# Rotary embedding on one core: all loads and stores in one ring, the end of each load run as a DMA of its own

## The chip, the core and the metric

The kernel runs on one core of one Trainium2 chip. The metric is the time of one execution in microseconds (us) on the device; several executions are taken and their median is given. One further execution was profiled; every line of the profile comes from it.

## The reference

The input `x` has 16 batches of 512 rows of 1024 float32 numbers; a row holds 16 heads of 64. `cos` and `sin` are tables of 512 x 32. Every head is rotated by the angles of its row:

```python
x = x.reshape(batch, seq, num_heads, head_dim)
x1, x2 = x[..., :half_dim], x[..., half_dim:]
rotated = np.concatenate([x1 * cos - x2 * sin, x1 * sin + x2 * cos], axis=-1)
```

The result is float32 and as large as `x`: 33.55 MB are read and as many written.

## The kernel before, in words

**Tiling.** The work is cut into 8 slabs of 4 MB (`nslabs`). A slab is two half batches: each of the 128 partitions holds 8 consecutive rows (`rpp`), so 8192 float32 numbers or 32 KB (`W` elements) a partition. Two slabs that follow each other share their two batches; in memory their 32 KB lie side by side, so two slabs can be moved by one DMA with 64 KB a partition. The on-chip tile `room` has 6 places for slabs (`slots`); slab `s` lies in place `s % 6`, so slab 6 takes the place of slab 0 and slab 7 that of slab 1.

**Computation, in place.** Every slab goes through five steps, in one pass or, for the first slab and the last two, in two passes of half a slab. ScalarE (ACT) casts float32 to bf16 into the lower half of the slab's own room (L146). VectorE (DVE) makes two products with the tables (L174), one of them with the halves of each head exchanged, and adds them (L177). ACT casts the sum back to float32 over the slab (L178). The slab is then ready to be stored. The tables are prepared once at the start, by small loads on ACT's queue (L89), a cast on GpSimd (L122), eight matmuls on TensorE (L130) and two copies by DVE (L135).

**Loads.** The dictionary `loads` names the DMAs: slabs 0 and 1 alone, slabs 2 and 3 together, slabs 4 and 5 together, slabs 6 and 7 alone. `load` (L70 to L73) issues those for slabs under 6 on SyncE's queue (SP, queue q1 of the profile), all four at the start. Slabs 6 and 7 are loaded from ACT's queue (q10 of the profile): ACT's program issues load 6 between its work for slabs 3 and 4, load 7 one slab later (`LATE = 3`), and each waits until the slab that had the place, 0 or 1, has landed in memory as output.

**Stores.** `stores` names those: slabs 0, 1, 2, 3 alone, 4 and 5 together, 6 and 7 alone. L182 issues them on SP, each behind the last cast of its last slab. The first stands in SP's queue behind the four loads, which have been issued long before.

**Order.** ACT and DVE run in the order in which the program is written (`manual_schedule`); a cast of the next slab stands ahead of the work on the present one. SP's order before the change comes from the planner and is: loads 0, 1, 2, 4, then stores 0, 1, 2, 3, 4, 6, 7. In what follows a load or store is called by its first slab: load 4 is that of slabs 4 and 5.

**Words.** A DMA of 128 partitions is spread over the core's 16 DMA engines; each moves 8 of the 128 rows, and one such row (32 or 64 KB a partition) is one packet in the profile. A queue is a ring of such packets on every engine.

Of the kernel before, what the change touches and what calls it, by code (L numbers as in the profile page):

```python
# [2 lines left out]

# [4 lines left out]


@with_exitstack  # L10
def kernel(
    ctx: ExitStack,
    tc: tile.TileContext,
    x: bass.AP,
    cos: bass.AP,
    sin: bass.AP,
    num_heads: int,
    out: bass.AP,
):
    nc = tc.nc  # L20
    P = nc.NUM_PARTITIONS

    batch, seq, dim = x.shape
    nh = num_heads
    hd = dim // nh
    half = hd // 2
    bf16 = mybir.dt.bfloat16
    f32 = mybir.dt.float32

    nb = 2  # L30
    slots = 6
    LATE = 3
    nslabs = batch // nb
    G = 2
    rpp = nb * seq // P
    W = rpp * dim
    SP = seq // rpp
    TW = rpp * half

    out_flat = out.rearrange("b s h d -> b s (h d)")  # L40

    singles = ctx.enter_context(tc.tile_pool(name="singles", bufs=1))
    psum = ctx.enter_context(tc.tile_pool(
        name="psum", bufs=1, space=bass.MemoryType.PSUM))


    def dram(t, s, k):
        return bass.AP(tensor=t.tensor,
                       offset=t.offset + s // G * (G * nb * seq * dim) + s % G * W,
                       ap=[[G * W, P], [1, k * W]])  # L50


    def view(t, offset, *dims):
        return dataclasses.replace(t, offset=t.offset + offset,
                                   ap=[t.ap[0], *[list(d) for d in dims]])


    room = singles.tile([P, slots * W], f32, tag="room")
    halves = room.bitcast(bf16)


    def slab(s, k):
        return view(room, s % slots * W, (1, k * W))


    loads = {0: 1, 1: 1, 2: 2, 4: 2, 6: 1, 7: 1}
    stores = {0: 1, 1: 1, 2: 1, 3: 1, 4: 2, 6: 1, 7: 1}


    def load(s):  # L70
        k = loads[s]
        queue = nc.sync if s < slots else nc.scalar
        queue.dma_start(out=slab(s, k), in_=dram(x, s, k))  # L73

    TR = 32
    TQ = seq // TR // rpp
    TC = seq * half // TR
    raw = singles.tile([P, TC], f32, tag="raw")  # L80
    nc.vector.memset(raw, 0.0)  # L81


    def load_tables(queue):
        for i, src in enumerate((cos, sin)):
            to = dataclasses.replace(
                raw, offset=raw.offset + i * raw.ap[0][0],
                ap=[[P // TR * raw.ap[0][0], TR], [1, TC]])
            queue.dma_start(out=to, in_=bass.AP(  # L89
                tensor=src.tensor, offset=src.offset, ap=[[TC, TR], [1, TC]]))  # L90


    load(0)
    load_tables(nc.scalar)
    for s in loads:
        if 0 < s < slots:
            load(s)

    GP = SP // G
    GT = G // TQ
    pick = singles.tile([P, 3 * GT * P], bf16, tag="pick")
    nc.gpsimd.memset(pick, 0.0)  # L104


    def selection(g, h):
        return pick[:, (g * GT + h // TQ) * P:(g * GT + h // TQ + 1) * P]


    for g in range(3):
        for h in range(0, G, TQ):
            part = view(selection(g, h), 0, (GP, P // GP), (1, GP))
            nc.gpsimd.affine_select(  # L114
                out=part, in_=part, compare_op=mybir.AluOpType.not_equal,
                fill=-1.0 if g == 2 else 1.0,
                base=-(1 if g else 0) - h // TQ * (P // TR),
                pattern=[[0, P // GP], [-(G // TQ) * (P // TR), GP]],
                channel_multiplier=1)

    raw_b = singles.tile([P, TC], bf16, tag="raw_b")
    nc.gpsimd.tensor_copy(out=raw_b, in_=raw)  # L122

    tab = {}


    def table(h):
        acc = psum.tile([P, 2 * rpp * hd], f32, tag=f"acc{h}")
        for g, at in ((0, 0), (0, half), (2, rpp * hd), (1, rpp * hd + half)):
            nc.tensor.matmul(  # L130
                view(acc, at, (hd, rpp), (1, half)), selection(g, h),
                view(raw_b, h % TQ * TW, (half, rpp), (1, half)),
                start=True, stop=True)
        tab[h] = singles.tile([P, 2 * rpp * hd], bf16, tag=f"tab{h}", name="tab")
        nc.vector.tensor_copy(out=tab[h], in_=acc)  # L135

    def span(u):
        s, r, n = u
        at, m = s % slots * W + r * dim, n * dim
        return (m, view(room, at, (1, m)), view(halves, 2 * at, (1, m)),  # L140
                view(halves, 2 * at + m, (1, m)))


    def cast(u):
        m, full, low, high = span(u)
        nc.scalar.copy(out=low, in_=full)  # L146

    passes = []
    for s in range(nslabs):
        n = rpp if 1 <= s < nslabs - 2 else rpp // 2
        passes += [(s, r, n) for r in range(0, rpp, n)]


    with tc.manual_schedule(engines={mybir.EngineType.Activation, mybir.EngineType.DVE}):
        cast(passes[0])
        done = 1
        for i, u in enumerate(passes):  # L160
            s, r, n = u
            if i == 0:
                for h in range(G):
                    table(h)
            ahead = len(passes[:rpp // passes[0][2]]) if i == 0 else i + 1
            for v in passes[done:ahead + 1]:
                cast(v)
            done = max(done, ahead + 1)
            if s - LATE + slots in loads and s >= LATE and r == 0:
                load(s - LATE + slots)  # L170
            m, full, low, high = span(u)
            turned = view(low, half, (hd, n * nh), (-half, 2), (1, half))
            for out_, in_, a in ((high, turned, rpp * hd), (low, low, 0)):
                nc.vector.tensor_mul(  # L174
                    out=out_, in0=in_,
                    in1=view(tab[s % G], a + r * hd, (hd, n), (0, nh), (1, hd)))
            nc.vector.tensor_add(out=high, in0=low, in1=high)  # L177
            nc.scalar.copy(out=full, in_=high)  # L178
            if r + n == rpp:
                for t, k in stores.items():  # L180
                    if t + k - 1 == s:
                        nc.sync.dma_start(out=dram(out_flat, t, k), in_=slab(t, k))  # L182


# [1 line left out]
_INS = ['x', 'cos', 'sin', 'num_heads']  # L186
_OUTS = [((16, 512, 16, 64), 'float32')]

_NUMBERS = {'num_heads': 16}


# [26 lines left out]
```

## Time and profile before

| what | value |
|---|---|
| median of 3 executions | 162.21 us (162.21 to 162.39) |
| the profiled execution's own time | 162.0 us |
| its span in the profile | 160.2 us |
| bytes read and written in device memory | 33.69 and 33.55 MB |

The span goes from the first to the last instruction; 1.8 us lie outside of it. In the profile SPq and ACTq are the parts of those engines that issue DMAs; "to landing" is the time from a DMA's issue until all its data has arrived and its semaphore says so. The view of stretches gives, for a stretch of the span, each engine's busy time, then TensorE's clock, the mean busy share of the 16 DMA engines, and GB/s. It books a packet wholly where it begins, so in short stretches the share can be over 1.

### The profile page before, as it was taken

What the parts mean: (1) busy time and instruction counts of PE and PEld (TensorE: products, weight loads), DVE (VectorE), ACT (ScalarE), POOL (GpSimd) and SP (SyncE); (2) the same over time, 40 slices, a digit from 0 to 9 for tenths busy, and PEclk for the clock granted to TensorE, in tenths of its full rate; (3) what the DMA queues carried; (4) which work ended last, traced back from release to release, by engine and by line L of the source; (5) the groups of instructions that cost most, each with busy time, mean ns of one, the idle gap of its engine ahead of it and who ended that gap; (6) DMA issues with size and microseconds to landing.
All of it is one profiled execution on the core that took longest, in us unless ns stands there. A gap on an engine that the chain in (4) does not pass through costs nothing.

```text
span 160.2 us, 170 instructions
## 1 busy us (share of the span) xinstructions
PE 1.9 (1%) x8; PEld 1.1 (1%) x8; DVE 110.1 (69%) x36; ACT 113.2 (71%) x23; POOL 2.1 (1%) x9
## 2 busy tenths in 40 slices
PE   0004000000000000000000000000000000000000
PEld 0002000000000000000000000000000000000000
DVE  1002999999906998999899899997399999000000
ACT  3006939992499999999999999299999991800000
POOL 3001000000000000000000000000000000000000
DMA  7999999979989996999999999999998998999994
GB/s 262 409 409 393 515 401 524 458 327 524 425 360 524 409 376 270 458 450 401 458 450 393 450 466 393 442 442 425 417 532 360 524 409 376 401 458 450 393 442 213
DMA packets 1968, 67.24 MB, mean 420 GB/s; under 512 B 240, under 2 KB 240, under 8 KB 304
## 3 DMA queue, kind: packets, MB, share of 16 engines
q1 hardware_dynamic: 1584, 58.72, 85.8%
q10 hardware_dynamic: 384, 8.52, 12.3%
HBM read 33.69 MB, written 33.55 MB: 420 GB/s over the span
## 4 chain that ended last, share of the span: by engine, by line
ACT 36%; DMA 25%; DVE 21%; issue 4%; SPq 1%; ACTq 0%
DMA room<-in_x_dram 25%; ACT room L178 20%; ACT room L146 17%; DVE room L174 14%; DVE room L177 7%; SPq L73 1%; ACTq L178 0%
## 5 line engine op out<-in xcount | busy, mean ns | idle before, releaser
L174 DVE TENSOR_TENSOR room<-room,tab 128x4096 bf16<-128x4096 bf16 (+1 forms) x22 | 71.7, 3260 | 10.9 <-ACT room L146 10.5
L146 ACT CAST room<-room 128x4096 bf16<-128x4096 f32 (+1 forms) x11 | 56.6, 5155 | 17.1 <-DMA room<-in_x_dram 17.1
L178 ACT CAST room<-room 128x4096 f32<-128x4096 bf16 (+1 forms) x11 | 56.6, 5156 | 6.6 <-DVE room L177 6.6
L177 DVE TENSOR_TENSOR room<-room 128x4096 bf16<-128x4096 bf16 (+1 forms) x11 | 35.9, 3262 | 0.4
L135 DVE CAST tab<-acc 128x1024 bf16<-128x1024 f32 x2 | 2.4, 1219 | 13.6 <-PE acc L130 13.6
L146 ACT ACT_TABLE_LOAD x1 | 1.3, 1283 | 2.6 <-issue 2.6
L130 PE MATMUL acc<-raw_b,pick 128*128 128x256 bf16 x8 | 1.9, 415 | 13.9 <-POOL raw_b L122 13.9
L130 PEld LDWEIGHTS <-pick 128*128 128x128 bf16 x8 | 1.1, 140 | 14.2 <-issue 12.3
L81 DVE MEMSET raw<- 128x512 f32 x1 | 0.5, 485 | 0.9 <-PEq L199 0.9
L114 POOL TENSOR_SCALAR_AFFINE_SELECT pick<-pick 128x128 bf16<-128x128 bf16 x3 | 0.8, 309 | 0.1
L122 POOL CAST raw_b<-raw 128x512 bf16<-128x512 f32 x1 | 0.6, 611 | 11.2 <-DMA raw<-in_sin_dram 11.2
L104 POOL MEMSET pick<- 128x384 bf16 x1 | 0.4, 418 | 0.3 <-POOLq L199 0.3
L199 POOL MEMSET const-float32-0.0<- 128x1 f32 x1 | 0.1, 99 | 0.2 <-issue 0.2
L199 POOL MEMSET const-bfloat16-1.0<- 128x1 bf16 x1 | 0.1, 102 | 0.0
L199 POOL MEMSET const-uint8-127<- 128x1 uint8 x1 | 0.1, 102 | 0.0
L199 POOL MEMSET const-float32-1.0<- 128x1 f32 x1 | 0.1, 99 | 0.0
## 6 DMA issues: line engine op xcount, KB each, us to landing
out_dram<-room SPq DMA_DIRECT2D x6, 4096.0 KB, 33.6
room<-in_x_dram SPq DMA_DIRECT2D x2, 4096.0 KB, 17.1
room<-in_x_dram ACTq DMA_DIRECT2D x2, 4096.0 KB, 24.8
raw<-in_cos_dram ACTq DMA_DIRECT2D x1, 64.0 KB, 7.9
raw<-in_sin_dram ACTq DMA_DIRECT2D x1, 64.0 KB, 11.1
room<-in_x_dram SPq DMA_DIRECT2D x2, 50.5
out_dram<-room SPq DMA_DIRECT2D x1, 28.7
```

The lines of the kernel that those rows point to most:

```text
L73: queue.dma_start(out=slab(s, k), in_=dram(x, s, k))
L81: nc.vector.memset(raw, 0.0)
L104: nc.gpsimd.memset(pick, 0.0)
L114: nc.gpsimd.affine_select(out=part, in_=part, compare_op=mybir.AluOpType.not_equal, fill=-1.0 if g == 2 else 1.0, base=-(1 if g else 0) - ...
L122: nc.gpsimd.tensor_copy(out=raw_b, in_=raw)
L130: nc.tensor.matmul(view(acc, at, (hd, rpp), (1, half)), selection(g, h), view(raw_b, h % TQ * TW, (half, rpp), (1, half)), start=True, sto ...
L135: nc.vector.tensor_copy(out=tab[h], in_=acc)
L146: nc.scalar.copy(out=low, in_=full)
L174: nc.vector.tensor_mul(out=out_, in0=in_, in1=view(tab[s % G], a + r * hd, (hd, n), (0, nh), (1, hd)))
L177: nc.vector.tensor_add(out=high, in0=low, in1=high)
L178: nc.scalar.copy(out=full, in_=high)
L199: nc = _bacc.Bacc("TRN2", target_bir_lowering=False, num_devices=1)
```

## The change

There is no load on ACT's queue any more: all loads and stores of slabs are issued on SP, whose order is now written out too. Loads 0, 1, 2 and 4 are issued first, then stores 0 and 1, then loads 6 and 7, then the other stores.

Loads 4 and 7, the last ones ahead of a store, are cut in two DMAs. The last two rows, 2048 numbers or 8 KB a partition (`TAIL = 2`), are a DMA of their own, 1 MB in all. The store behind each of them (store 0 behind load 4, store 2 behind load 7: `gates`) gets a wait: it is issued only when the first part of that load has landed. The tail's DMA is in the queue by then. Load 6 waits for store 0 to land and load 7 for store 1, as before, but now on SP. The work of ACT, DVE, TensorE and GpSimd is the same, but for the two DMA issues that leave ACT.

```diff
-    LATE = 3
+    TAIL = 2
...
+    gates = {4: 0, 7: 2}
+    opened = {}
+
+    def piece(t, s, a, b):
+        return bass.AP(tensor=t.tensor,
+                       offset=t.offset + s // G * (G * nb * seq * dim) + s % G * W + a,
+                       ap=[[G * W, P], [1, b - a]])
 
     def load(s):
-        k = loads[s]
-        queue = nc.sync if s < slots else nc.scalar
-        queue.dma_start(out=slab(s, k), in_=dram(x, s, k))
+        end = loads[s] * W
+        cut = end - TAIL * dim if s in gates else end
+        for a, b in ((0, cut), (cut, end)):
+            if a < b:
+                done = nc.sync.dma_start(
+                    out=view(room, s % slots * W + a, (1, b - a)),
+                    in_=piece(x, s, a, b))
+                if s in gates and a == 0:
+                    opened[gates[s]] = done.ins
+
+    def store(s):
+        gone = nc.sync.dma_start(out=dram(out_flat, s, stores[s]), in_=slab(s, stores[s]))
+        if s in opened:
+            tc.add_manual_dep(
+                gone.ins, opened[s].name,
+                mybir.DependencyInfo(mybir.DependencyClass.Sync,
+                                     mybir.DependencyReason.DATA),
+                reason="behind the load")
...
-    with tc.manual_schedule(engines={mybir.EngineType.Activation, mybir.EngineType.DVE}):
+    with tc.manual_schedule(engines={
+            mybir.EngineType.Activation, mybir.EngineType.DVE, mybir.EngineType.SP}):
...
-            if s - LATE + slots in loads and s >= LATE and r == 0:
-                load(s - LATE + slots)
...
-                        nc.sync.dma_start(out=dram(out_flat, t, k), in_=slab(t, k))
+                        store(t)
+                if s == 1:
+                    load(6)
+                    load(7)
```

## The prediction

> **What bounds the kernel now.** I read the page's totals first, then its chain, then how full the DMA engines are in chosen stretches, because the totals point to them.
>
> ```profile
> span 160.2 us, 170 instructions
> PE 1.9 (1%) x8; PEld 1.1 (1%) x8; DVE 110.1 (69%) x36; ACT 113.2 (71%) x23; POOL 2.1 (1%) x9
> ...
> DMA packets 1968, 67.24 MB, mean 420 GB/s; under 512 B 240, under 2 KB 240, under 8 KB 304
> q1 hardware_dynamic: 1584, 58.72, 85.8%
> q10 hardware_dynamic: 384, 8.52, 12.3%
> ACT 36%; DMA 25%; DVE 21%; issue 4%; SPq 1%; ACTq 0%
> ```
>
> No compute engine is over 71% busy, but the two queues together fill 98.1% of the 16 DMA engines' time. The chain names ACT first, which misleads: it follows the last cast back, and that cast only has to be done before the queue gets to its store. So I checked how long the last store lay in the queue. The first rows are the time-ordered view and the view of the store's line, both near the end; then stretches, whose last two columns are the mean busy share of a DMA engine and GB/s. A packet is booked wholly in the stretch where it begins, so share times width is the mean length of the one packet per engine that begins there, and GB/s times width is their bytes.
>
> ```profile
> 136.01 3.61 ACT L178 CAST room<-room 128x4096 f32<-128x4096 bf16 x1 [3.56 <-DVE room L177]
> 139.64 0.33 SPq L182 DMA_DIRECT2D out_dram<-room  x1
> DMA to landing us min/median/max: 19.7/19.7/19.7
> ...
> core 0: us, PE busy (x) PEld busy (x) DVE busy (x) ACT busy (x) POOL busy (x), PEclk, DMA share, GB/s
> 62.70:110.00 47.30, 0.00 (x0) 0.00 (x0) 45.61 (x12) 44.27 (x8) 0.00 (x0) 1.00 1.00 433
> 110.00:156.00 46.00, 0.00 (x0) 0.00 (x0) 21.63 (x10) 26.00 (x8) 0.00 (x0) 1.00 1.00 433
> ```
>
> The last store, 4.19 MB, is issued at 139.64 and needs 4.19/0.433 = 9.7 us of engine time, yet lands 19.7 us later: about 10 us lie behind other stores. Compute therefore has some 10 us of cover, and the end is set by the queue. From 62.7 on it moves 433 GB/s without a hole, in the stretch where the two rings mix (62.7 to 110) as in the one with stores alone. 67.24 MB at 433 GB/s are 155.3 us; what is left of 160.2 is start, end, and anything lost between. Only a loss between can be won back.
>
> ```profile
> 1.75:2.20 0.45, 0.00 (x0) 0.00 (x0) 0.00 (x0) 0.00 (x0) 0.30 (x2) 1.00 4.22 1165
> 41.30:41.45 0.15, 0.00 (x0) 0.00 (x0) 0.15 (x1) 0.00 (x0) 0.00 (x0) 1.00 1.01 437
> 41.75:41.90 0.15, 0.00 (x0) 0.00 (x0) 0.15 (x1) 0.00 (x0) 0.00 (x0) 1.00 1.01 437
> 55.90:56.30 0.40, 0.00 (x0) 0.00 (x0) 0.40 (x1) 0.40 (x2) 0.00 (x0) 1.00 6.05 2621
> 58.30:58.80 0.50, 0.00 (x0) 0.00 (x0) 0.50 (x1) 0.50 (x1) 0.00 (x0) 1.00 6.87 2097
> 58.80:61.50 2.70, 0.00 (x0) 0.00 (x0) 2.70 (x1) 2.70 (x1) 0.00 (x0) 1.00 0.00 0
> 61.50:62.30 0.80, 0.00 (x0) 0.00 (x0) 0.80 (x1) 0.80 (x1) 0.00 (x0) 1.00 1.53 655
> ...
> 2.11 0.68 SPq L73 DMA_DIRECT2D room<-in_x_dram  x1
> DMA to landing us min/median/max: 60.4/60.4/60.4
> ```
>
> The loss is there. The 16 second-to-last packets of load 4 (64 KB each) begin at 55.9 to 56.3 and take 6.05 x 0.40 = 2.42 us. The last 16 begin at 58.3 to 58.8 and take 6.87 x 0.50 = 3.44 us, and store 0's first packets follow (61.5 to 62.3). So the one **turn from load to store in a ring costs 3.44 - 2.42 = 1.02 us**. It is the load that ends late: issued at 2.11, it lands 60.4 later, at 62.5. The turn from load 2 to load 4 shows nothing of the kind: its packets begin one per 0.15 us from 41.4 to 41.9, and the 2.42 us rhythm goes on.
>
> **The change part by part.** Times are added to the profiled run (162.0 us, 1.8 outside the span); the median is 162.21, so I add the difference to the median.
>
> *Loads 6 and 7 go from ACT's ring to SP's.* Two issues leave ACT, which had cover. The question is what mixing the rings had cost. The next rows are the DMA view of 76.0 to 76.9, where load 6 gets in between the stores, the issue of that load, and that of store 2.
>
> ```profile
> DMA packets 16, 0.52 MB, mean 583 GB/s; under 512 B 0, under 2 KB 0, under 8 KB 0
> q10 hardware_dynamic: 16, 0.52, 134.8%
> ...
> 72.28 0.34 ACTq L73 DMA_DIRECT2D room<-in_x_dram  x1
> L182 SPq DMA_DIRECT2D out_dram<-room x1: 332/332/332, 70.0 to 70.0; - x1
> ```
>
> The first load packet of each engine on the second ring takes 1.348 x 0.9 = 1.21 us for 32 KB, which is the full rate: a turn between rings costs nothing. So unmixing gains 0, and what had been free turns become turns inside a ring: store 1 to load 6 (new), load 7 to store 2 (new), beside load 4 to store 0 (old). By the Trainium skill, "DMA: Bandwidth & Descriptors", section "Issuing engines are not separate DMA queues", the issuing engine only saves issue time; the 433 GB/s on both sides agree, but that rule would price a turn inside a ring at nothing too, and the 1.02 us here say otherwise.
>
> *Store to load inside a ring (about 81 us).* Not shown. Bounds: 0 (the turn between rings, just read) and the start from nothing, where the first packets take 4.22 x 0.45 = 1.90 us for 32 KB instead of 1.21, so 0.7. I take 0, since there too a store stood before the load; a gain is excluded, as the engines are already full.
>
> *What waits on SP.* Its compiled order is now loads 0, 1, 2, 4 and tail, stores 0 and 1, loads 6, 7 and tail, stores 2 on. Load 6 waits for store 0 to land, which is when it was issued before too (72.28); load 7 for store 1, 9.7 us later; store 2 for the first 24 KB a partition of load 7, 9.7 + 7.3 us after that, at about 99. Behind them stand all stores from 2 on, of which the first was issued at 70.0. No slab reuses their slots, and the ring is never empty before: store 1, load 6 and load 7 keep it filled in turn. Compute stays early: store 7 is issued at about 139.6, and the ring gets to it at about 150. Cost 0; cover some 10 us.
>
> *The tails.* 8 KB a partition are 8 packets of 8 KB per engine, 64 KB or 2.42 us at the rate above. What small packets cost is bounded by the DMA view from 6 to 12.4, where the tables come in rows of 2 KB:
>
> ```profile
> q1 hardware_dynamic: 80, 2.62, 94.8%
> q10 hardware_dynamic: 80, 0.13, 5.4%
> ```
>
> 5.4% of 16 x 6.4 us over 80 packets (a fifth of them without data) is 0.07 us each, and the two rings fill 100.2%: close to the full rate. I take 0.05 for both tails together; bounds 0 and 0.2.
>
> *The gates.* Store 0 has stood in the ring since 36.9; now it comes when the first part of load 4 has landed. When does it reach the engines? The chain, in order of time, shows a landing and the wait that it ends:
>
> ```profile
> 1.65 40.55 DMA room<-in_x_dram
> 42.20 0.02 issue
> 42.22 2.14 ACT room L146
> ...
> 0.74 2.06 SPq L73 DMA_DIRECT2D room<-in_x_dram  x4
> 0.70:1.75 1.05, 0.00 (x0) 0.10 (x1) 0.48 (x1) 0.00 (x0) 0.95 (x4) 1.00 0.00 0
> 36.93 0.35 SPq L182 DMA_DIRECT2D out_dram<-room  x1
> ```
>
> Load 2's last packets end as load 4's first begin, 41.4 to 41.9, and it has landed at 42.20, 0.4 after the slowest. Load 4's first part is 56 KB a packet: 7/8 of 2.42 x 8 = 16.9 us, so it ends at 58.35 to 58.7, has landed at 59.1, and the store is issued at 59.13. The very first load, issued at 0.74, has no packet before 1.75 and all 16 begun by 2.20: from issue to packet 1.0 us on the first engine, at most 1.45 on the last; so the store arrives at 60.15 to 60.6. The tail would end at 60.8 to 61.15. Thus the store is **no longer 22 us early but about 0.6 us** (60.95 - 60.37), and no engine runs dry.
>
> What does the turn then cost? My reading of the late landing: the store's reads of the on-chip memory, in the ring behind the load, take a share of the path on which the load's last data come in. The Trainium skill, same page, section "Two DMAs through the same engine are not ordered", says that an engine's read and write sides are separate and pipelined; that fits a store reading before the load has ended, and no run yet shows it. A store that comes 0.6 us before the end can then delay it by 0.6 at most if it shares evenly, by 0 if it starts slowly, and by the whole 1.02 if its read-ahead goes first. Bounds 0 and 1.02 for each turn; I take 0.6, the overlap.
>
> **Sum:** -1.02 (old turn) + 0.6 (load 4 to store 0) + 0.6 (load 7 to store 2) + 0 (store to load) + 0.05 (tails) = +0.23 us; 162.0 becomes 162.2 in a profiled run, 162.21 becomes **162.4**. By this sum alone the change is worth nothing either way: what each gate wins, the second turn in the ring takes back.
>
> **The rivals.**
>
> *Clean turns.* The store's first reads come so late that the load isn't delayed: each turn costs 0 to 0.2. For it: the tail covers the way from landing to arrival with only 0.6 to spare, and a slower issue than 1.0 us brings it closer. Against: the arrival row. -1.02 + 0.1 + 0.05 = -0.9: 161.3.
>
> *Each turn at the full price (slower).* What costs is that a store follows a load in a ring with no gap, however late it came; or the read-ahead fills its 1.02 us first. Place: 61 and 101 us. It decides as soon as the store arrives before the load's last data, which the times above say it does. +1.02 + 0.05 (tails) = +1.07: 163.3. For it: a single turn, seen once, at that price. Against: a load that lands late has been delayed by something concurrent, and the gate cuts the time in which that can act.
>
> *The gate opens too late.* If a landing or an arrival took more than the 2.42 us of the tail, the engines idle at both turns. From the rows it takes 0.4 + 1.0 to 1.45, plus the 0.35 between fastest and slowest engine, 1.8 to 2.2 us; beyond 2.42 every 0.1 us costs 0.2. The only longer way from issue to packet in the trace is load 6's, 72.28 to about 76, 3.8 us, behind packets of the other ring. With the middle of 1.0 and 3.8, 2.4 us, the engines idle 0.4 + 0.35 + 2.4 - 2.42 = 0.75 us at each turn, and the store's first packets may lose up to the 0.7 of the start: 2 x (0.75 to 1.45) - 1.02 = +0.5 to +1.9, 162.7 to 164.1. The Trainium skill, same page, section "Anatomy of one DMA — SWDGE (gpsimd) path", puts most of a fixed 2 us on the receipt after the last byte; the 0.4 us here speak against it.
>
> That the change does not do what it says I give no chance: the waits stand in SP's compiled order.
>
> **How the numbers follow.** Half-price turns (the sum) 36%, from 0.3 to 0.9 a turn: 161.8 to 163.0. Clean turns 26%: 161.1 to 161.8. Full price 26%: 162.9 to 163.7. Gate too late: 8%, 162.7 to 164.1. The sum with the store-to-load turn at its 0.7: 4%, 163.1. A range of 161.1 to 163.7 leaves out the late gate's upper part and what lies beyond the cases' edges; I allow 15% for these. A measurement of this kernel can tell about 0.2%, 0.32 us, from no change. Faster by more (under 161.89): the clean turns and 5 points of the sum's case, 31%. Within: 22 points of the sum's case. Slower: 9 points of the sum's case, 26, 8 and 4, 47%. The forecast is the single likeliest case, though slower holds more in all.
>
> **What would show it.** In the profile after: the tail's last packets at about 61 and 101 us (length over 0.30 us for 8 KB is the turn's price); load 4's tail landing near 62.1 (sum), 61.5 (clean) or 62.5 (full price); store 0 issued at 59.1; a stretch without packets between tail and store (gate too late); first packets of load 6, near 81, over 1.21 us (store to load). If the engines stop for compute after 110, the cover was misread and the forecast is wrong.

## The result, and the profile after

| | median us | executions | ratio to before, 95% interval |
|---|---|---|---|
| before | 162.21 (161.98 to 162.39) | 22 | |
| changed kernel | 161.69 (161.32 to 162.81) | 22 | 0.9976 (0.9966 to 0.9986) |

The median fell by 0.52 us (0.32%); the ratio, in which the changed kernel's long upper side counts, says 0.24%. No change was forecast (162.4). The profiled execution took 161.81 us; 162.0 before.

The page of the changed kernel first: the load of the DMA engines is as high as before (97.6 + 0.2 = 97.8%), but the second queue holds the two tables only.

```profile
span 160.0 us, 176 instructions
DMA packets 2256, 67.24 MB, mean 420 GB/s; under 512 B 272, under 2 KB 272, under 8 KB 336
q1 hardware_dynamic: 2160, 67.11, 97.6%
q10 hardware_dynamic: 96, 0.13, 0.2%
```

Next, in order of time, the issue of store 0, and from the view of the loads' line the tail of load 4, issued at 2.8:

```profile
59.17 0.35 SPq L91 DMA_DIRECT2D out_dram<-room  x1
L83 SPq DMA_DIRECT2D room<-in_x_dram x1: 586/586/586, 2.8 to 2.8; - x1
DMA to landing us min/median/max: 58.8/58.8/58.8
```

Store 0 is issued at 59.17 (59.13 was worked out). The tail lands at 2.8 + 58.8 = 61.6, so load 4 arrives whole 0.9 us sooner than the 62.5 of before.

For what is lost at a turn I use one reading throughout. At the full rate the 16 engines move 433 GB/s, so in a stretch of width w the time by which an engine's packets are longer than their bytes need is **w x (share - GB/s / 433)**. The rounding leaves it uncertain by some 0.03 us; 128 tail packets of 8 KB add 0.06. The stretches around the first turn (58 to 63), the turn back to loads (78 to 84) and the second turn (97 to 103), of the kernel before:

```profile
58.00:63.00 5.00, 0.00 (x0) 0.00 (x0) 4.59 (x2) 5.00 (x2) 0.00 (x0) 1.00 1.02 354
78.00:84.00 6.00, 0.00 (x0) 0.00 (x0) 5.96 (x2) 6.00 (x2) 0.00 (x0) 1.00 1.00 431
97.00:103.00 6.00, 0.00 (x0) 0.00 (x0) 5.96 (x2) 4.20 (x2) 0.00 (x0) 1.00 1.00 431
```

and of the changed kernel, with four narrower ones:

```profile
58.00:63.00 5.00, 0.00 (x0) 0.00 (x0) 4.53 (x2) 5.00 (x2) 0.00 (x0) 1.00 0.99 419
60.77:61.14 0.37, 0.00 (x0) 0.00 (x0) 0.37 (x1) 0.37 (x1) 0.00 (x0) 1.00 3.47 1484
78.00:84.00 6.00, 0.00 (x0) 0.00 (x0) 5.97 (x2) 6.00 (x2) 0.00 (x0) 1.00 0.95 393
78.90:79.40 0.50, 0.00 (x0) 0.00 (x0) 0.50 (x1) 0.50 (x1) 0.00 (x0) 1.00 2.79 1049
97.00:103.00 6.00, 0.00 (x0) 0.00 (x0) 5.97 (x2) 4.13 (x2) 0.00 (x0) 1.00 1.02 436
156.30:157.20 0.90, 0.00 (x0) 0.00 (x0) 0.00 (x0) 0.00 (x0) 0.00 (x0) 1.00 1.35 583
157.20:157.90 0.70, 0.00 (x0) 0.00 (x0) 0.00 (x0) 0.00 (x0) 0.00 (x0) 1.00 0.11 47
```

Before, the first turn costs 5 x (1.02 - 354/433) = 1.01 us, and the two later places 0.03. After, the first turn costs 5 x (0.99 - 419/433) = 0.11, most of it the tail's small packets: store 0's first packets (with three of the tail's, 60.77 to 61.14) take the time that their bytes need. The second turn costs 0.08, again the tail. What is new is the turn back to loads: 6 x (0.95 - 393/433) = 0.25. It starts with store 1's last packets, 78.90 to 79.40: 2.79 x 0.50 = 1.40 us each instead of 1.21. That is a mean over the engines. One engine lost more there; its packets can be followed, as each begins where the one before ends:

```profile
79.27:79.29 0.02, 0.00 (x0) 0.00 (x0) 0.02 (x1) 0.02 (x1) 0.00 (x0) 1.00 5.15 1638
80.93:80.95 0.02, 0.00 (x0) 0.00 (x0) 0.02 (x1) 0.02 (x1) 0.00 (x0) 1.00 4.57 1639
82.38:82.40 0.02, 0.00 (x0) 0.00 (x0) 0.02 (x1) 0.02 (x1) 0.00 (x0) 1.00 4.17 1638
```

In each of these stretches a single packet of 33 KB begins; 16 x 0.02 x share gives 1.65, 1.46 and 1.33 us, together 0.8 more than three times 1.21. The rows at the end fit that: 16 packets begin from 156.30 to 157.20, and after that a single one of 0.7 x 47 GB/s = 33 KB. One engine ends a good half microsecond behind the others and sets the end; that it is the same engine is likely, not shown. So of -1.01 + 0.11 + 0.25 + 0.08 = -0.57 us on average, this profiled execution shows -0.19 in its time, and the medians -0.52.

### The profile page after: what moved, and what is told of

Read it like the earlier page. It is cut to its first block, busy times and chain, and to the rows that moved or that the text cites. A ratio compares the mean times of both kernels' runs of the same rounds, so it can differ in the third digit from the quotient of the medians.

```text
span 160.0 us, 176 instructions
## 1 busy us (share of the span) xinstructions
PE 1.9 (1%) x8; PEld 1.1 (1%) x8; DVE 110.1 (69%) x36; ACT 113.2 (71%) x23; POOL 2.1 (1%) x9
## 3 DMA queue, kind: packets, MB, share of 16 engines
q1 hardware_dynamic: 2160, 67.11, 97.6%
## 4 chain that ended last, share of the span: by engine, by line
ACT 45%; DMA 25%; DVE 13%; issue 4%; SPq 0%; ACTq 0%
DMA room<-in_x_dram 25%; ACT room L201 24%; ACT room L170 20%; DVE room L197 8%; DVE room L200 4%; SPq L83 0%; ACTq L201 0%; ACTq L170 0%
```

## The experiments

All times are medians, beside executions of the kernel before on the same chip (162.21 to 162.24 in all three groups). What the turns cost is worked out by the formula above, from one profiled execution of each kernel, which need not be a typical one: those of e4 (162.71) and e8 (161.97) were the fastest of their kernel, those of e1 (162.95), e10 (162.67) and e11 (163.45) the slowest. The prices are means over the engines, while the engine that ends last sets the time, so their sums do not give the times: e12's come to 0.85 against 1.07 before, yet its profiled execution took 162.37 against 162.0.

| kernel | us | ratio, 95% interval | first turn | back to loads | second turn |
|---|---|---|---|---|---|
| before | 162.2 | | 1.01 | 0.03, two rings | 0.03, two rings |
| changed | 161.69 | 0.9976 (0.9966 to 0.9986) | 0.11 | 0.25 | 0.08 |
| e1: cut, no gates | 162.51 | 1.0024 (1.0013 to 1.0034) | 1.16 | 0.03 | 0.32 |
| e2: plain ring | 162.41 | 1.0015 (1.0006 to 1.0023) | 1.14 | 0.05 | 0.19 |
| e4: two rings, first gate | 163.18 | 1.0063 (1.0047 to 1.0078) | 0.11 | 0.37 + 0.82, two rings | two rings |
| e5: tail of 4 rows | 162.39 | 1.0015 (1.0007 to 1.0024) | 1.08 | 0.03 | 0.14 |
| e8: load 6 gated too | 162.22 | 1.0007 (0.9992 to 1.0021) | 0.11 | 0.68 | 0.06 |
| e9: first gate only | 162.24 | 1.0025 (0.9999 to 1.0051) | 0.11 | 0.23 | 0.68 |
| e10: second gate only | 162.41 | 1.0013 (1.0005 to 1.0022) | 1.36 | 0.03 | 0.14 |
| e11: tail of 1 row | 163.34 | 1.0065 (1.0052 to 1.0078) | idle | 0.91 | idle |
| e12: tail of 3 rows | 162.28 | 1.0005 (0.9996 to 1.0013) | 0.79 | 0.00 | 0.06 |
| e13: changed again | 161.74 | 0.9971 (0.9960 to 0.9981) | 0.06 | 0.25 | 0.08 |

### The first four: gate or cut, and where the rest goes

Theory A held that the store's early place in the ring is what costs, theory B that the load's large last packets do.

**e1: both cuts, no waits.**

```diff
-        if s in opened:
+        if False:
```

> One ring with the two tails as DMAs of their own, but without the two waits. Theory A (a store that stands in the ring long before the load ends delays it; the gate is what helps): both turns cost 1.0 us again, tail packets over 0.31 us near 61 and 101, load 4's tail lands near 62.5 instead of 61.56; 161.7 + 2 x 1.0 = 163.5 to 163.9. Theory B (the small packets at the end of the load are what helps, as little of the load is in flight beside the store; the gate does nothing): both turns stay clean, the tail lands at 61.5; 161.5 to 161.9.

```profile
58.00:63.00 5.00, 0.00 (x0) 0.00 (x0) 4.59 (x2) 5.00 (x2) 0.00 (x0) 1.00 0.96 315
78.00:84.00 6.00, 0.00 (x0) 0.00 (x0) 5.97 (x2) 6.00 (x2) 0.00 (x0) 1.00 1.00 431
97.00:103.00 6.00, 0.00 (x0) 0.00 (x0) 5.97 (x2) 4.20 (x2) 0.00 (x0) 1.00 1.01 414
L83 SPq DMA_DIRECT2D room<-in_x_dram x1: 559/559/559, 2.8 to 2.8; - x1
DMA to landing us min/median/max: 60.0/60.0/60.0
```

162.51 us. In the first stretch the engines begin 315 GB/s worth of packets where the changed kernel had 419, at the same share: 1.16 us lost, and the tail lands at 62.8, not 61.6. The packets are as small as in the changed kernel, so **B falls: the wait is what helps, not the cut**. But A's sum was too high: the second turn costs 0.32, not 1.0, and the turn back to loads, 0.25 in the changed kernel, costs nothing here.

**e2: one ring, neither cut nor wait.**

```diff
-    gates = {4: 0, 7: 2}
+    gates = {}
```

> One ring without cut and without waits. Both theories: each turn from load to store costs the 1.02 us seen before the change, last load packets of 3.44 us at 58.4 and of 2.2 us (32 KB) near 100, and the turn from store to load near 80.5 costs its 0.25 mean and 0.8 on the slowest engine; 161.7 + 2.0 = 163.3 to 163.9. If the turns cost less here than 1.0 each, the price isn't a constant of the turn.

```profile
58.00:63.00 5.00, 0.00 (x0) 0.00 (x0) 4.61 (x2) 5.00 (x1) 0.00 (x0) 1.00 0.97 321
78.00:84.00 6.00, 0.00 (x0) 0.00 (x0) 5.97 (x2) 6.00 (x2) 0.00 (x0) 1.00 0.98 421
97.00:103.00 6.00, 0.00 (x0) 0.00 (x0) 5.97 (x2) 4.21 (x2) 0.00 (x0) 1.00 0.99 415
```

162.41 us, some 1 us under what was expected: 1.14 at the first turn, 0.05 back to loads, 0.19 at the second. The price is not a constant of the turn. The plain ring is only 0.2 us slower than the two rings, about what its second turn lost.

**e4: the kernel before, with cut and wait at load 4 only.**

```diff
-    gates = {4: 0, 7: 2}
+    gates = {4: 0}
...
-                done = nc.sync.dma_start(
+                done = (nc.sync if s < slots else nc.scalar).dma_start(
...
+            if s - LATE + slots in loads and s >= LATE and r == 0:
+                load(s - LATE + slots)
```

> Kernel before (loads 6 and 7 on ACT's ring) with the cut and the wait at load 4 only. If the changed kernel lost its last part at the turn from store to load inside the ring (0.25 us mean, 0.8 on the slowest engine), this one has no such turn and no second turn from load to store: 162.2 - 1.1 + 0.07 = 161.1 to 161.3, with less spread than the changed kernel. If the loss near 80.5 comes from elsewhere, it stays: 161.6 to 161.8. Theories A and B both: the turn near 61 is clean.

```profile
58.00:63.00 5.00, 0.00 (x0) 0.00 (x0) 4.63 (x2) 5.00 (x1) 0.00 (x0) 1.00 0.99 419
74.00:78.00 4.00, 0.00 (x0) 0.00 (x0) 3.50 (x2) 4.00 (x2) 0.00 (x0) 1.00 1.00 393
84.00:90.00 6.00, 0.00 (x0) 0.00 (x0) 5.96 (x2) 6.00 (x1) 0.00 (x0) 1.00 1.07 404
```

163.18 us, the clearest miss: 161.1 to 161.3 was expected, and it was to be the best version. The gated turn is as clean as hoped (0.11). But mixing the rings, which had cost nothing before the change, now costs 4 x (1.00 - 393/433) = 0.37 where load 6 begins and 6 x (1.07 - 404/433) = 0.82 ten microseconds later, about when store 1 ends in the other ring (load 7, which waits for it, is issued at 88.71). What the gate saved was taken back, and more. This is what forms **theory C: the first store behind a load buys the engines a lead of reading over writing, about 1 us, which lasts as long as they stay busy; loads that come later need it, and where a gate has avoided the purchase, they pay.** Its rival, **theory D**: each gate saves a turn's price, and the turn back to loads has a price of its own.

**e5: tails of 4 rows.**

```diff
-    TAIL = 2
+    TAIL = 4
```

> As the changed kernel, but the tail is 4 rows, 16 KB a partition, 4.83 us a tail. The stores are issued about 2.4 us earlier relative to the load's end, so they arrive about 3 us before it. Theory A with a price that grows with the overlap up to 1.02: both turns at the full price, 161.7 + 2.0 = 163.3 to 163.9. Theory B (packets of 16 KB instead of 8, gate without effect): turns stay nearly clean, 161.5 to 162.2.

```profile
58.00:63.00 5.00, 0.00 (x0) 0.00 (x0) 4.56 (x2) 5.00 (x2) 0.00 (x0) 1.00 1.04 357
```

162.39 us. A gate that lets the store in 2.4 us sooner is worth nothing: 1.08 at the first turn. A's mechanism is right, and once the first turn is paid, the rest is again nearly free (0.03, 0.14). When the delay begins can be read too. First e1, the issue of store 0 and two stretches, then the same of e5:

```profile
36.95 0.35 SPq L91 DMA_DIRECT2D out_dram<-room  x1
55.00:58.60 3.60, 0.00 (x0) 0.00 (x0) 3.56 (x2) 3.60 (x2) 0.00 (x0) 1.00 0.61 257
58.60:61.10 2.50, 0.00 (x0) 0.00 (x0) 2.50 (x1) 2.50 (x1) 0.00 (x0) 1.00 1.06 262
56.80 0.35 SPq L91 DMA_DIRECT2D out_dram<-room  x1
57.70:58.60 0.90, 0.00 (x0) 0.00 (x0) 0.86 (x2) 0.90 (x1) 0.00 (x0) 1.00 1.11 473
58.60:61.50 2.90, 0.00 (x0) 0.00 (x0) 2.90 (x1) 2.90 (x1) 0.00 (x0) 1.00 1.01 282
```

By the formula e1 loses 0.06 before 58.6 and 1.14 after it, e5 0.02 and 1.04. In e1 the store has been in the ring since 36.95, in e5 it comes about a microsecond before 58.6, and in both the load's packets are longer only from 58.6 on. A store that is there still sooner delays nothing more, so the 4 rows cost as much as no gate.

### The next four: does a price that was not paid come back?

**e6 and e7: no loads behind the first store, with gate and without.**

```diff
-    loads = {0: 1, 1: 1, 2: 2, 4: 2, 6: 1, 7: 1}
+    loads = {0: 1, 1: 1, 2: 2, 4: 2}
...
-    gates = {4: 0, 7: 2}
+    gates = {4: 0}
...
-                if s == 1:
-                    load(6)
-                    load(7)
```

e7 has `gates = {}`.

> The changed kernel without loads 6 and 7 (left out: the last two slabs rotate slabs 0 and 1 a second time), so that after load 4's gated tail there are stores only. Less to move: 8.4 MB, 19.3 us. Theory C (a store behind a load buys the engines a lead of reading over writing, about 1 us, at the load's expense; the lead lasts, and later loads use it; a gate avoids the purchase, and the next load then pays): nothing later asks for the lead, so no packet is longer than its share anywhere after 5 us, and the kernel ends 1.0 to 1.1 us before the next one, which has no gate. Theory D (the loss near 80 belongs to a turn from store to load as such, the gate simply removes the price of a turn from load to store): the same here; with the next two runs it tells how much of the gate's gain is kept.

> The same without cut and gate (loads 6 and 7 left out too). Both theories: load 4's last packets take 1.0 us more, nothing else; ends 1.0 to 1.1 us after the one with the gate.

154.17 and 154.28 us. Between the ends 1.0 to 1.1 us was expected, and 0.11 came. The ends say little: with two loads less the ring runs empty ahead of store 4, which waits for its casts, and that hole swallows what was gained. So I compare where store 3 lands, ahead of the hole. First the view of the stores' line with the gate:

```profile
L91 SPq DMA_DIRECT2D out_dram<-room x1: 333/333/333, 83.9 to 83.9; - x1
DMA to landing us min/median/max: 16.4/16.4/16.4
```

then without, and its first turn:

```profile
L91 SPq DMA_DIRECT2D out_dram<-room x1: 332/332/332, 83.8 to 83.8; - x1
DMA to landing us min/median/max: 17.7/17.7/17.7
58.00:63.00 5.00, 0.00 (x0) 0.00 (x0) 4.51 (x2) 5.00 (x2) 0.00 (x0) 1.00 0.97 315
```

With the gate store 3 lands at 83.9 + 16.4 = 100.3, without at 101.5: 1.2 us, the whole price of the ungated turn (5 x (0.97 - 315/433) = 1.21). With no later load, nothing is paid back.

**e8: load 6 gated as well.** Store 1 is cut like a load, and load 6 is issued when its first part has landed.

```diff
+        if s == 1:
+            cut = W - TAIL * dim
+            for a, b in ((0, cut), (cut, W)):
+                part = nc.sync.dma_start(out=piece(out_flat, s, a, b),
+                                         in_=view(room, s % slots * W + a, (1, b - a)))
+                if a == 0:
+                    opened["load 6"] = part.ins
+            return
...
+                if s == 6:
+                    tc.add_manual_dep(done.ins, opened["load 6"].name,
...
```

> The changed kernel with one gate more: store 1's last 8 KB a partition are an own DMA, and load 6 is issued when the rest of store 1 has landed, so that it reaches the engines as the store ends, not 9 us before. Theory D with the gate's mechanism (what stands in the ring behind other work delays it): the loss near 80.5 (0.25 mean, 0.8 slowest) goes, 161.0 to 161.3. Theory C: no lead is there to hide the way of load 6's first data, and a later issue can't help; the loss stays or grows to the 0.6 to 0.7 of the first packets of the run, 161.6 to 162.4.

```profile
78.00:84.00 6.00, 0.00 (x0) 0.00 (x0) 5.97 (x2) 6.00 (x2) 0.00 (x0) 1.00 1.09 423
```

162.22 us: the turn back to loads grows from 0.25 to 6 x (1.09 - 423/433) = 0.68, which is C's 0.6 to 0.7 and the opposite of D's. A store gains from coming late, a load does not.

**e9: the first gate only.**

```diff
-    gates = {4: 0, 7: 2}
+    gates = {4: 0}
```

> The changed kernel with the first cut and gate only; store 2 stands behind an uncut load 7. Theory C: the lead was partly bought near 80.5, so the second turn costs the rest, 0.2 to 0.8 (the ungated ones cost 0.18 and 0.27 after a first turn of 1.1 to 1.3): 161.9 to 162.5. Theory D: the second turn costs a turn's full 1.0: 162.7.

```profile
58.00:63.00 5.00, 0.00 (x0) 0.00 (x0) 4.63 (x2) 5.00 (x1) 0.00 (x0) 1.00 0.99 419
78.00:84.00 6.00, 0.00 (x0) 0.00 (x0) 5.96 (x2) 6.00 (x2) 0.00 (x0) 1.00 0.92 382
97.00:103.00 6.00, 0.00 (x0) 0.00 (x0) 5.96 (x2) 4.24 (x2) 0.00 (x0) 1.00 1.01 388
```

162.24 us. The ungated second turn costs 0.68. In e1 and e2, where the first turn had been paid, the same turn cost 0.32 and 0.19. So its price depends on what was paid before, as C has it. And the second gate is worth 0.5 us (162.24 against 161.69): without it the changed kernel gains nothing. Its 12 times lie in two groups, eight from 161.90 to 162.41, the profiled one among them, and four from 163.40 to 164.39; what those four paid for, no profile shows.

### The last four: the other gate, the timing, and the changed kernel again

**e10: the second gate only.**

```diff
-    gates = {4: 0, 7: 2}
+    gates = {7: 2}
```

> The changed kernel with the second cut and gate only; store 0 stands behind an uncut load 4. Theory C (the lead of reading over writing): the first turn pays 1.0 to 1.2, the turn back to loads near 81 is then free, and the gated second turn pays 0 instead of the 0.18 to 0.27 of an ungated one: 162.1 to 162.3. Theory D (each gate saves one turn's price, whatever came before): 161.7 + 1.0 with the 0.25 at 81 kept: 162.7.

```profile
58.00:63.00 5.00, 0.00 (x0) 0.00 (x0) 4.54 (x2) 5.00 (x2) 0.00 (x0) 1.00 1.00 315
78.00:84.00 6.00, 0.00 (x0) 0.00 (x0) 5.97 (x2) 6.00 (x2) 0.00 (x0) 1.00 1.00 431
97.00:103.00 6.00, 0.00 (x0) 0.00 (x0) 5.97 (x2) 4.14 (x2) 0.00 (x0) 1.00 1.01 427
```

162.41 us, a little over C's range (162.1 to 162.3). The profiled execution, the slowest of its eleven, paid 1.36 at the first turn, where C had 1.0 to 1.2. The turn back to loads is free, as C has it; D's 0.25 is not there. With e2, e9 and the changed kernel this fills the square: no gate 162.41, first 162.24, second 162.41, both 161.7. Only both together gain.

**e11: tails of 1 row**, so that the store comes 1.2 us later (`TAIL = 1`).

> The changed kernel with tails of 1 row, 4 KB a partition, 1.23 us. The stores are then issued about 1.2 us later relative to the load's end. In the changed kernel they came just in time (first packets right behind the tail, none longer), so here the engines should stand idle at both turns, by up to 1.2 us each less the slack that the changed kernel had: 162.0 to 164.0, and gaps without packets behind both tails.

```profile
60.91 0.35 SPq L91 DMA_DIRECT2D out_dram<-room  x1
60.91:61.76 0.85, 0.00 (x0) 0.00 (x0) 0.85 (x1) 0.85 (x1) 0.00 (x0) 1.00 0.76 308
61.76:61.95 0.19, 0.00 (x0) 0.00 (x0) 0.19 (x1) 0.19 (x1) 0.00 (x0) 1.00 6.09 2587
78.00:84.00 6.00, 0.00 (x0) 0.00 (x0) 5.97 (x2) 6.00 (x1) 0.00 (x0) 1.00 0.96 350
```

163.34 us. The engines run dry, and that measures the way from issue to packet: issued at 60.91, store 0 has 0.19 x 2587 GB/s = 0.49 MB, 15 packets, begin from 61.76 on, **0.85 us later**. After the dry spell the turn back to loads costs 0.91.

**e12: tails of 3 rows** (`TAIL = 3`).

> The changed kernel with tails of 3 rows, 12 KB a partition, 3.65 us. The stores arrive about 1.2 us earlier than in the changed kernel, 1.2 later than with 4 rows. Theory C with a price that grows with the time by which the store is early: the first turn costs 0.3 to 0.7, and the turn near 81 less than 0.25, in part paid already: 161.6 to 162.2. If being early at all costs the whole lead, the first turn costs 1.0 and the rest nothing: 162.2 to 162.5.

```profile
58.07 0.35 SPq L91 DMA_DIRECT2D out_dram<-room  x1
58.00:63.00 5.00, 0.00 (x0) 0.00 (x0) 4.61 (x2) 5.00 (x1) 0.00 (x0) 1.00 1.08 399
78.00:84.00 6.00, 0.00 (x0) 0.00 (x0) 5.97 (x2) 6.00 (x2) 0.00 (x0) 1.00 1.01 437
```

162.28 us: 0.79 at the first turn, nothing after it. The hope for a small lead at a small price failed; being early by one row costs nearly the whole.

**e13: the changed kernel once more**, without an edit.

> The changed kernel once more, for a second profiled execution: the excess near 80 should be there again (0.2 to 0.6 mean over the engines, up to 0.5 to 1.3 on the slowest), the two gated turns clean again; time 161.3 to 162.8 with the spread that its 22 runs showed. If the excess near 80 is different while the time of the execution moves with it, that turn makes the spread.

```profile
78.00:84.00 6.00, 0.00 (x0) 0.00 (x0) 5.97 (x2) 6.00 (x2) 0.00 (x0) 1.00 1.00 415
```

161.74 us (161.37 to 162.08), the same gain, and the same 0.25 in its profile; both profiled executions took 161.8, so they do not show why the changed kernel's times spread more than those of before. The other runs say where the spread belongs. It is wide in kernels that gate the first turn and load later (the changed kernel 161.32 to 162.81, e4 162.71 to 163.63, e8 161.97 to 163.50, e9 161.90 to 164.39) and narrow in those that pay at the first turn (before 161.98 to 162.39; e1, e2, e5, e10 and e12 within 0.63 each). It is narrowest in e6, which gates the first turn and loads nothing later (154.14 to 154.21 in four executions). What differs from one execution to the next stays open. No version tried beats the changed kernel.

## Why the prediction was wrong, point by point

- **What bounds the kernel: right.** The end follows the DMA engines; the 10 us of cover for compute were never used up except in e6 and e7, which have less to move.
- **The old turn at 1.02 us: right**, and its reading too: the load is what is late, because the store stands behind it. e1, e2, e5, e7 and e10 show it again at 1.08 to 1.36. The Trainium skill's rule that an engine's read and write sides are separate and pipelined ("DMA: Bandwidth & Descriptors", "Two DMAs through the same engine are not ordered") fits this, but no run shows the two sides apart.
- **The moment at which the store arrives: right.** 1.0 to 1.45 us after the issue were taken, 0.85 to 1.0 measured (e11). So in the changed kernel store 0, issued at 59.17, arrives from 60.0 on, some 0.8 us ahead of the tail's end (60.77 to 61.14); I had 0.6. What I held the 0.4 us from last packet to landing against is stated for DMAs that GpSimd issues, and none here is.
- **"I take 0.6, the overlap" for each turn: this step failed.** It measured 0.05 and 0.02 beside the tail's own 0.06. The cost does not grow evenly with the overlap: a store that comes about 0.8 us before the load's end costs nothing (changed kernel), one of about 2 us 0.79 (e12: issued at 58.07, there from 58.9 on), one of about 3 us 1.08 (e5). One that has been there for 22 us costs no more, as its delay falls wholly into the load's last 2.4 us (e1, from 58.6 on). A packet of a load seems to be booked as ended about 1 us after its reading is over, so that a store which comes within that time finds nothing to delay; that is argued from these points, not shown. The lower bound of 0 came true, though not shown for the reason given ("if it starts slowly"). With it came the rival of the clean turns (161.1 to 161.8, 26%), in part by luck: it rested on a store that comes later than worked out, which it did not, and 161.69 lies near its upper end because of the next point.
- **The turn back to loads at 0: the second miss.** 0.25 on average, and 0.8 on one engine. My reason, that a turn between rings had been free, was drawn from a kernel that had paid its first turn. e4 shows the same turn between rings at 0.37 + 0.82 when that payment is missing. The upper bound of 0.7 holds for e8 (0.68), not for e11 (0.91).
- **The tails at 0.05 for both: too low**, 0.06 each.
- The sum with measured terms: -1.01 + 0.11 + 0.25 + 0.08 = -0.57 instead of +0.23, which with 162.21 gives 161.6; measured 161.69. That the two agree so well is partly luck: the terms come from an execution that took 161.81, only 0.19 less than the one of before.
- **"Each turn at the full price"** was not even true of the plain ring (e2): 1.14 and 0.19. The rival took the price for a constant of the turn.
- **What moving the loads to SP's ring costs: half right.** I let the rule of the Trainium skill ("DMA: Bandwidth & Descriptors", "Issuing engines are not separate DMA queues"), that the issuing engine only saves issue time, stand with a price of 0 for the ring. With the first turn paid that holds within 0.2 us (e2 against before). With the first turn gated it does not: the same loads cost 0.25 in SP's ring (e9 and the changed kernel) and 1.19 in ACT's (e4).

**What is shown and what is argued.** Shown: the wait, not the cut, makes the first turn clean (e1); paid once, the later places cost 0 to 0.3 (e1, e2, e5, e10, e12); not paid, later loads or an ungated turn pay 0.2 to 1.2 (changed kernel, e4, e8, e9); with no later loads the gate's 1.2 us are kept (e6 against e7). That what is bought is a lead of reading over writing is a reading that foretold e8, e9 and the free turn of e10; the inside of an engine isn't seen. No run sets that lead against another state of the engines that a paid turn could leave behind. Why the unpaid lead costs 0.25 in one ring and 1.19 in two stays open.

## What to carry to other kernels

When a queue is full throughout, look for packets that are longer than their bytes need, and ask which of them paid for something that later ones use: a stall that is removed can come back at the next place that lived on it, as in e4. A store behind a run of loads is best issued so that it reaches the engines within the last microsecond of the load: here 2.4 us of tail did it, 3.6 us lost nearly all of the gain, 1.2 us let the engines run dry. Gates have to be tried in all their combinations, since either one alone gained nothing.

## What the runs showed of the hardware that I had not expected

- A load's last packets are delayed by a store that reaches the engines 2 us or more before their end (0.8 to 1.4 us), and not by one that comes 0.8 us before (0.05).
- The price of a turn depends on what came before: the same ungated turn from load 7 to store 2 cost 0.19 and 0.32 after an ungated first turn, 0.68 after a gated one.
- Two rings that alternate at the full rate (0.03 lost from 78 to 84 before the change) did so after such a stall; without it they lost 1.19 us (e4).
- From issue to first packet on engines that had run dry: 0.85 us.
